# Fox-gMLP trunk, one core: attention's first loads placed inside the last chunk, key weights split earlier, sums and forget rows one tile later

## The chip, the cores and the metric

The kernel runs on one core of one Trainium2 chip. The metric is the device time of one execution in microseconds (us). Before the change the median of three timed runs was 2390.56 us (2388.26 to 2390.97).

A core has five engines that run their own instruction queues: TensorE (PE, matmuls), VectorE (DVE), ScalarE (ACT), GpSimd (POOL) and SyncE (SP). SP computes nothing here; it issues transfers. An engine takes its instructions strictly in the order of its own queue, and waits on semaphores for others.

## The reference

One pre-norm layer for 2048 tokens of width 1024, in float32, and a last RMS norm. What matters here is its first half:

```python
xn = rms_norm(x, mix_norm_g)
h = xn @ w_in                       # 1024 x 2568
q, k, v, f_logit, z = split(h)      # 512, 512, 512, 8, 1024 wide; 8 heads of 64
log_f = log_sigmoid(f_logit + b_f)
c = cumsum(log_f)                   # per head, along the tokens
logit[t, s] = q_t . k_s / 8 + c[t] - c[s],   s <= t
attn = softmax(logit) @ v
sgu  = spatial_gating(gelu(z))      # 128-token chunks
x = x + concat(rms_norm(attn), rms_norm(sgu)) @ w_out
x = x + (silu(gate) * up) @ w_down  # a SwiGLU layer behind it, width 2816
```

## The kernel before

**Precision.** A float32 operand is held as two parts, a rounded one (`h`) and the remainder (`l`). A product is three matmuls: h by h, h by l, l by h. The rounded part of a weight comes from an ACT cast (`wh`, L128), the remainder from a DVE subtraction (`wl`, L131).

**Stage 1** makes q, k, v and the forget gates, for four chunks of 512 tokens. In a chunk, 16 matmuls make the forget logits (L539), then come four query tiles, four key tiles (24 matmuls each, L566, a pair of heads in each) and four value tiles (L460). Chunk 0 has its value tiles first, ahead of the forget logits. ACT, DVE and SP evacuate each tile: scaled, split, and stored to DRAM as `QH`, `QL`, `KH`, `KL`, `VD`. Three generators are advanced once or twice per tile, and what they issue goes between the matmuls:

- `steps` of the next chunk: its x is loaded, split, squared and summed; then `sums` (L285: four matmuls with one column each, that read the summed squares `rb`; DVE and POOL make 1/sqrt of them) and `row` (four transposes, L295).
- `forget_rows`: the chunk's forget logits go through DRAM (`FD`, L549, to the tile `F`), then ACT and DVE make log-sigmoid in the tile `v` (L323 to L331), a transpose (L335), a cumulative sum by matmul (L341), a carry (L345), and a store to `AUG`.
- `max_stream`: row maxima of the logits, ahead of attention. For a head, a chunk of queries and a chunk of keys, four matmuls (L363: tile `D` with keys and AUG rows, tile `A` with queries) and DVE maxima (L365). `D` has four buffers, and its loads run three jobs ahead. The maxima are stored by SP as `md`.

**Stage 2** is attention, mixed with the z projection (L921). A unit is one head and one chunk of queries; a step is one block of 128 keys against it: scores (L729, L730), exp on ACT (L732), p by v (L762 to L767). Its tiles: `load_keys` fills C (KH, KL), D (KH and ten AUG rows) and V; `prep` fills A and B (queries; A also takes the maxima `md`). The remaining `max_stream` runs on in stage 2. The big projections and the SwiGLU layer (L1654) follow.

**What sets the order.** A list scheduler orders every engine's queue when the program is built; `behind(x)` forbids it to place an instruction ahead of x. All loads of stage 2, all loads of `max_stream`, and the stores QL, KL and md are issued by SP, in one queue; POOL loads weights. Before, the first two units' keys and queries were one block behind `k_low[1]`, the store of the last chunk's second key tile:

```python
with behind(k_low[1]):
    for n, u in enumerate(units[:AHEAD]):
        keys_until(0)
        prep(*u, ab)
prep(*units[AHEAD], ab)
xz_in = [ldr(xz0[a], XS[0][:, a, :, 0:P]) for a in range(2)]
```

`xz_in` are the two loads `wsth`, `wstl` for the z projection. `jk` is the buffer for the constant rows `c_row`, which reach DRAM as `CR` and the constant rows of `AUG`; `cm` and `dmask` are constant matrices.

Of the kernel before, what the change touches and what calls it, by code (L numbers as in the profile page):

```python
# [16 lines left out]
P = 128  # L17
# [8 lines left out]
CH = 512  # L26
# [45 lines left out]
FT = 9  # L72
ND = 4
FE = 4
NCH = S // CH
NB = S // P
EPS = 1e-6
# [3 lines left out]
def f(ap):  # L81
    return ap.bitcast(F32)
# [3 lines left out]
def trunk(ctx: ExitStack, tc: tile.TileContext, x, x_t, mix_g, w_in, b_f, ln_g, ln_b, w_st, b_st, on_g, w_out,  # L86
# [55 lines left out]
    tri = cm[:, 0, :]  # L142
    dmask = T(csm, [P, CH], F32, "dmask")

    def load_mats():
        ld(cm, c_mat[:, 128:768].rearrange("p (n q) -> p n q", n=5))
        ld(dmask, c_mat[:, 768:1280])

    ones_c = T(cst, [P, 1], F32, "ones_c")
    onc = T(cst, [P, KT], F32, "onc")  # L150
# [80 lines left out]
    nc.scalar.activation(T(p1, [P, 4], F32, "r1a"), mhalf, AF.Copy, scale=ones_c)  # L231
    CR = T(dram, [34, CH], F32R, "CR")

    def load_const():
        cr = T(p1, [34, CH], F32, "jk", bufs=1)
        ld(cr, c_row)
        crr = T(p1, [34, CH], F32R, "D", bufs=ND)
        nc.vector.tensor_copy(crr, cr)
        ldr(CR, crr)
        a8, a2 = T(p1, [P, 8, P], F32R, "xl", bufs=4), T(p1, [P, 2, P], F32R, "D", bufs=ND)  # L240
        nc.gpsimd.memset(f(a8), 0.0)
        nc.gpsimd.memset(f(a2), -1.0)
        ldr(AUG[:, 0:8, :], a8)
        ldr(AUG[:, 8:10, :], a2)

    class Chunk:
# [51 lines left out]
        def steps(self):  # L298
            self.get(0)
            self.get(1)  # L300
            yield
            for i in range(4):
                self.halves(i)
                self.square(i)
                if i < 2:
                    self.get(i + 2)
                yield
            self.sums()
            yield
            self.row()  # L310
            yield
# [4 lines left out]
    def forget_rows(j):  # L316
# [12 lines left out]
        nc.vector.tensor_tensor(er, er, ru, ALU.mult)  # L329
        nc.vector.tensor_tensor(ln, ln, er, ALU.subtract)  # L330
        nc.vector.scalar_tensor_tensor(lf, F, 0.0, ln, ALU.min, ALU.subtract)  # L331
        for _ in range(2 if j < 2 else 1):
            yield
        pl = T(ps1, [P, 4, P], F32, "tp")
        nc.tensor.transpose(pl[:, 0, :], lf, ident)  # L335
# [112 lines left out]
        return nc.scalar if c else nc.sync  # L448

    last_v = []  # L450
    k_low = deque(maxlen=4)

    def v_open():
        return T(ps1m, [P, CH], F32, "mm", bufs=4)
# [7 lines left out]
    def v_close(pm, xc, tt):  # L462

        v = T(p1, [P, H, P + 1], F32R, "v") if xc.c else T(p1, [P, H, P + 1], F32R, "xh", bufs=4)
        r = r1[:, xc.c * 4 + tt : xc.c * 4 + tt + 1]
        pmv = pm.rearrange("p (h d) -> p h d", h=H)
        (nc.vector if xc.c == NCH - 1 else nc.gpsimd).memset(f(v[:, :, DH : DH + 1]), 1.0)
        a = nc.scalar.activation(v[:, :, 0:DH], pmv, AF.Copy, scale=r)
        nc.vector.scalar_tensor_tensor(v[:, :, P : P + 1], pmv[:, :, 0:1], r, f(v[:, :, 0:1]), ALU.mult, ALU.subtract)
        b = nc.vector.scalar_tensor_tensor(v[:, :, DH + 1 : P], pmv[:, :, 1:DH], r, f(v[:, :, 1:DH]), ALU.mult, ALU.subtract)  # L470
        s = queue(xc.c if xc.c < NCH - 1 or tt < 2 else 0).dma_start(f(VD[xc.c][tt * P : (tt + 1) * P]), f(v))
        if xc.c == NCH - 1 and tt == 1:

            nc.scalar.activation(T(p1, [P, 4], F32, "r1a"), f(v[:, 0, 0:4]), AF.Exp)
        return a, b, s
# [52 lines left out]
            nxt.row()  # L528
    for tt in range(4):
        closed = v_close(pms[tt], nxt, tt)  # L530
    for c in range(NCH):
        xc = nxt
        xh, xl = xc.hi, xc.lo
# [13 lines left out]
        nc.vector.tensor_tensor(fT, fT, xc.rb[0:8], ALU.mult)  # L547
        nc.scalar.activation(fT, fT, AF.Identity, bias=bfc)
        nc.scalar.dma_start(FD[c], fT)  # L549
        gates_ = forget_rows(c)  # L550
        next(gates_)
        n_early = -(-(4 * c * HE[c - 1] + 2) // EB[c]) if c else 0
# [4 lines left out]
        for which, w in ((0, wq), (1, wk)):  # L557
            for pr in range(4):
# [13 lines left out]
                if which == 0:  # L572
                    a = nc.scalar.mul(qh, qs, 0.125)
                    b = nc.vector.scalar_tensor_tensor(ql, qs, 0.125, f(qh), ALU.mult, ALU.subtract)
                    queue(c).dma_start(f(QH[pr][c]), f(qh))
                    s = ldr(QL[pr][c], ql)
                else:
                    a = hi_of(nc.scalar, qh, qs)
                    b = lo_of(nc.vector, ql, qs, qh)
                    queue(c).dma_start(f(KH[pr][c]), f(qh))  # L580
                    s = ldr(KL[pr][c], ql)
                    k_low.append(s)
                if c == which == pr == 0:
                    with behind(a, b, closed[2]):
                        load_mats()
                        load_const()
                        halves_k(0)
                        get_k(2)
                        halves_k(1)
                        get_k(3)  # L590
                if which == (c == 0):
                    xc.keep(pr, b)
                if c == which == 0:
                    with behind(a, b, closed[2]):
                        if pr == 1:
                            halves_k(2)
                        if pr == 2:
                            halves_k(3)
                if c == NCH - 1 and which and pr:
                    with behind(a, b):  # L600
                        halves_z(pr - 1)
# [611 lines left out]
            load_keys(*u, i)  # L1213

    with tc.high_priority():
        with behind(k_low[1]):
            for n, u in enumerate(units[:AHEAD]):
                keys_until(0)
                prep(*u, ab)
        prep(*units[AHEAD], ab)  # L1220
        xz_in = [ldr(xz0[a], XS[0][:, a, :, 0:P]) for a in range(2)]
    zc = z_consts()
    next(zc)
    zg = gates()
# [6 lines left out]
    for n in range(len(steps) + DEPTH):  # L1231
        if n < len(steps):
            h, j, kb = steps[n]
            keys_until(n)
            if n and kb == 0 and units.index((h, j)) + AHEAD < len(units):
                prep(*units[units.index((h, j)) + AHEAD], ab)
            max_due(steps[min(n + 3, len(steps) - 1)][0:2])
# [478 lines left out]
```

## Time and profile before

| | us |
|---|---|
| median of three timed runs | 2390.56 |
| the profiled execution | 2384.64 |
| its span, first to last instruction | 2382.8 |
| PE busy | 2338.7 (98%) |
| DVE busy | 1671.5 (70%) |
| ACT busy | 1055.9 (44%) |
| POOL busy | 627.4 (26%) |
| mean granted TensorE clock | 0.995 of full speed |

Busy is the time in which an engine had an instruction running. The timeline view has one row for an instruction or a group: start, duration, engine, line, operation, output and inputs, and in brackets how long the engine had been idle before, and which instruction ended that wait. The view by windows gives for each stretch the busy time and the number of instructions of PE, its weight loads, DVE, ACT and POOL, then the granted clock, the mean busy share of the 16 DMA engines and GB/s. The view of waits sums an engine's idle times by what ended them: total, number, longest.

### The profile page before, as it was taken

Reading aid. Unit: us, or ns where it says so; the run is one execution under the profiler, and the core shown is the slowest. Engines: PE = TensorE matmul, PEld = TensorE weight load, DVE = VectorE, ACT = ScalarE, POOL = GpSimd, SP = SyncE. Lnnn points to the kernel's source line nnn. Section 1 sums busy time; section 2 is a strip of 40 time slices with the busy share of each in tenths; the row PEclk is TensorE's granted clock in tenths of the full one; section 3 lists DMA queues with packets and bytes.
Section 4 is the critical chain, followed back from the end, with each engine's and each line's share of the span. In section 5 each row is a group of like instructions: output and inputs, shape, how many; then the busy total and the mean of one; then the engine's idle time right before and its main releaser. Section 6 shows DMA issues by size and latency. Waiting matters only on the chain. (4 is left out here: it accounts for less than half of the span.)

```text
span 2382.8 us, 31420 instructions
## 1 busy us (share of the span) xinstructions
PE 2338.7 (98%) x10582; PEld 1893.8 (79%) x10582; DVE 1671.5 (70%) x2736; ACT 1055.9 (44%) x1770; POOL 627.4 (26%) x705
## 2 busy tenths in 40 slices
PE   9999999999999999999999999999999999999997
PEld 7777777777777767888888888788888878888886
DVE  6658658888888666567655656965555696696888
ACT  5322137777778766344323233432323242332433
POOL 1100002122111222221322323232322335364531
PEclk9999999999999999999999999999999999999999
DMA  7845567566587876666233232433232245455453
GB/s 256 286 154 202 196 210 196 165 164 178 154 222 234 225 224 172 211 223 201 71 89 89 80 95 75 153 85 89 72 89 81 81 140 187 167 185 202 152 188 148
DMA packets 358152, 380.60 MB, mean 160 GB/s; under 512 B 22292, under 2 KB 275924, under 8 KB 355432
## 3 DMA queue, kind: packets, MB, share of 16 engines
q1 hardware_dynamic: 342008, 335.36, 46.4%
q0 software_dynamic: 7616, 27.33, 3.3%
q10 hardware_dynamic: 8368, 15.91, 1.8%
q8 instruction: 85, 1.39, 0.2%
q14 instruction: 75, 0.61, 0.1%
HBM read 253.35 MB, written 125.18 MB: 159 GB/s over the span
## 5 line engine op out<-in xcount | busy, mean ns | idle before, releaser
L128 ACT CAST wh<-raw 128x512 fp32r<-128x512 f32 (+2 forms) x492 | 302.3, 621 | 752.7 <-PE pp L1654 607.9
L131 DVE TENSOR_TENSOR wl<-raw,wh 128x512 fp32r<-128x512 f32 (+2 forms) x496 | 374.9, 766 | 80.2 <-ACT wh L128 79.8
L1654 PE MATMUL pp<-wl,wh 128*128 128x512 f32 x1056 | 325.5, 389 | 1.4 <-ACT u L1409 1.2
L1654 PE MATMUL pp<-wh,wh 128*128 128x512 f32 x1056 | 325.3, 389 | 0.0
L1343 POOL TENSOR_TENSOR raw<-raw 128x512 f32<-128x512 f32 (+1 forms) x124 | 165.5, 1336 | 514.9 <-DMA raw<-in_w_gu_dram 334.9
L131 DVE TENSOR_TENSOR Pl<-Pt,Ph 128x512 fp32r<-128x512 f32 (+1 forms) x320 | 194.6, 613 | 79.1 <-ACT Ph L128 76.4
L1654 PEld LDWEIGHTS pp<-wl,wh 128*128 128x128 f32 x1056 | 198.0, 188 | 43.6 <-ACT u L1409 2.1
L1654 PEld LDWEIGHTS pp<-wh,wh 128*128 128x128 f32 x1056 | 198.2, 188 | 41.1
L732 ACT ACTIVATE Pt<-mx_ps 128x512 f32<-128x512 f32 (+1 forms) x320 | 169.3, 534 | 121.6 <-PE mx_ps L730 117.6
L1654 PE MATMUL pp<-wl,wl 128*128 128x512 f32 x528 | 205.7, 390 | 1.0 <-DVE wl L131 0.9
L1654 PE MATMUL pp<-wh,wl 128*128 128x512 f32 x528 | 205.4, 389 | 0.0
L921 PE MATMUL z<-wh,xz 128*128 128x512 f32 x496 | 188.9, 397 | 0.0
L1343 DVE TENSOR_TENSOR raw<-raw,raw 128x512 f32<-128x512 f32 (+1 forms) x112 | 133.8, 1197 | 77.4 <-POOL raw L1343 73.9
L128 ACT CAST Ph<-Pt 128x512 fp32r<-128x512 f32 (+1 forms) x320 | 175.8, 557 | 19.6 <-PE tp L764 3.8
L365 DVE TENSOR_REDUCE mx<-mx_ps 128x1 f32<-128x512 f32 x192 | 130.2, 682 | 23.9 <-PE mx_ps L363 20.4
L742 POOL TENSOR_SCALAR_AFFINE_SELECT Ph<-Ph 128x128 fp32r<-128x128 f32 x128 | 53.0, 414 | 323.0 <-DVE Pl L131 218.6
L363 PE MATMUL mx_ps<-D,A 66*128 66x512 f32 (+2 forms) x320 | 119.6, 376 | 5.7 <-DMA D<-KH 3.0
L762 PE MATMUL tp<-Ph,V 128*128 128x512 f32 (+1 forms) x320 | 118.6, 371 | 4.5 <-POOL Ph L742 3.6
L729 PE MATMUL mx_ps<-A,D 74*128 74x512 f32 (+1 forms) x320 | 118.9, 372 | 2.2 <-ACT Pt L732 2.2
L767 PE MATMUL tp<-Pl,V 128*128 128x512 f32 (+1 forms) x320 | 118.5, 370 | 1.2 <-POOL Pl L742 0.7
L1654 PEld LDWEIGHTS pp<-wl,wl 128*128 128x128 f32 x528 | 99.1, 188 | 22.6 <-DVE wl L131 2.1
L730 PE MATMUL mx_ps<-B,C 128*128 128x512 f32 (+1 forms) x320 | 116.9, 366 | 0.0
(340 smaller groups left out, 5300.9 us busy)
## 6 DMA issues: line engine op xcount, KB each, us to landing
raw<-in_w_gu_dram SPq DMA_DIRECT2D x88, 512.0 KB
xz<-XS SPq DMA_DIRECT2D x31, 1024.0 KB
HD<-hT SPq DMA_DIRECT2D x44, 512.0 KB
D<-KH SPq DMA_DIRECT2D x112, 128.0 KB
XA<-xa SPq DMA_DIRECT2D x27, 512.0 KB
raw<-HD SPq DMA_DIRECT2D x24, 512.0 KB
XA<-xb SPq DMA_DIRECT2D x21, 512.0 KB
xa<-XA SPq DMA_DIRECT2D x20, 512.0 KB
```

The lines of the kernel that those rows point to most:

```text
L128: return nc.scalar.copy(o, i) if eng is nc.scalar else eng.tensor_copy(o, i)
L131: return eng.tensor_tensor(o, i, f(h), ALU.subtract)
L363: last_mx.append(nc.tensor.matmul(pm[:, 0:n], lhs, Dt[0 : lhs.shape[0], 0:n], start=True, stop=True))
L365: nc.vector.tensor_reduce(mx[:, a, s : s + 1], pm, AX.X, ALU.max)
L729: nc.tensor.matmul(st[:, off:], Dt[:, b * P : (b + 1) * P], A[:, off:], start=True, stop=False)
L730: nc.tensor.matmul(st[:, off:], C[:, b * P : (b + 1) * P], B[:, off:], start=False, stop=True)
L732: nc.scalar.activation(Pt[:, off:], st[:, off:], AF.Exp)
L762: nc.tensor.matmul(pv[:, off:], V[:, 0:P], Ph[:, off:], start=kb == 0, stop=False)
L767: nc.tensor.matmul(pv[:, off:], V[:, 0:P], Pl[:, off:], start=False, stop=kb == 4 * j + 3)
L921: nc.tensor.matmul(pz, xz[a][:, k, :], w[b][:, k, :], start=n == 0, stop=n == 3 * KT - 1)
L1343: (nc.vector if e == "v" else nc.gpsimd).tensor_tensor(o, a, b, op)
L1654: nc.tensor.matmul(pm, a[:, k, :], b[:, k, :], start=on is None and k == 0 and e == 0, stop=k == it.kh - 1 and e == 2, skip_group_check=n ...
```

## The change

- **Early loads.** Every store of a query's or key's low part, and the last two value stores of the last chunk, are kept in `stores`; in the last chunk's numbering 0 to 3 are the query tiles, 4 to 7 the key tiles, 8 and 9 the third and fourth value tile. `EARLY` names a store for each load: the first unit's keys and queries stand behind the second query tile's store, the second unit's behind the fourth, the third unit's queries behind the second key tile's, `xz_in` behind the fourth key tile's. All other key loads of the first 32 steps stand behind the third value tile's store.
- **Key weights.** The splits of the first two pieces of the key weights, and the loads of the last two, go from behind chunk 0's first query tile to behind its second value tile.
- **Constants.** `cm` and `c_row` are loaded ahead of chunk 0's query tiles, `dmask` at its fourth query tile; the cast and the stores of `c_row` stay behind the first query tile.
- **One tile later.** Chunk 1's `sums` take one more step, and so does the transpose in chunk 0's forget rows.

```diff
+EARLY = [1, 3, 5, 7, 8]
...
-    def load_const():
-        cr = T(p1, [34, CH], F32, "jk", bufs=1)
-        ld(cr, c_row)
+    def store_const(cr):
         crr = T(p1, [34, CH], F32R, "D", bufs=ND)
         nc.vector.tensor_copy(crr, cr)
...
                 if i < 2:
                     self.get(i + 2)
                 yield
+            if self.c == 1:
+                yield
             self.sums()
...
-        for _ in range(2 if j < 2 else 1):
+        for _ in range((3, 2, 1, 1)[j]):
             yield
         pl = T(ps1, [P, 4, P], F32, "tp")
         nc.tensor.transpose(pl[:, 0, :], lf, ident)
...
-    k_low = deque(maxlen=4)
+    stores = deque(maxlen=10)
...
         s = queue(xc.c if xc.c < NCH - 1 or tt < 2 else 0).dma_start(f(VD[xc.c][tt * P : (tt + 1) * P]), f(v))
+        if xc.c == NCH - 1 and tt >= 2:
+            stores.append(s)
...
         closed = v_close(pms[tt], nxt, tt)
+        if tt == 1:
+            with behind(*closed[:2]):
+                halves_k(0)
+                get_k(2)
+                halves_k(1)
+                get_k(3)
...
         nc.scalar.dma_start(FD[c], fT)
+        if c == 0:
+            cr = T(p1, [34, CH], F32, "jk", bufs=1)
+            ld(cm, c_mat[:, 128:768].rearrange("p (n q) -> p n q", n=5))
+            ld(cr, c_row)
...
-                    s = ldr(QL[pr][c], ql)
+                    stores.append(ldr(QL[pr][c], ql))
...
-                    s = ldr(KL[pr][c], ql)
-                    k_low.append(s)
+                    stores.append(ldr(KL[pr][c], ql))
                 if c == which == pr == 0:
                     with behind(a, b, closed[2]):
-                        load_mats()
-                        load_const()
-                        halves_k(0)
-                        get_k(2)
-                        halves_k(1)
-                        get_k(3)
+                        store_const(cr)
...
                         if pr == 2:
                             halves_k(3)
+                        if pr == 3:
+                            ld(dmask, c_mat[:, 768:1280])
...
-        with behind(k_low[1]):
-            for n, u in enumerate(units[:AHEAD]):
-                keys_until(0)
+        for u, at in zip(units[:AHEAD], EARLY):
+            with behind(stores[at]):
+                load_keys(*u, loads.pop(0)[3])
                 prep(*u, ab)
-        prep(*units[AHEAD], ab)
-        xz_in = [ldr(xz0[a], XS[0][:, a, :, 0:P]) for a in range(2)]
+        with behind(stores[EARLY[2]]):
+            prep(*units[AHEAD], ab)
+        with behind(stores[EARLY[3]]):
+            xz_in = [ldr(xz0[a], XS[0][:, a, :, 0:P]) for a in range(2)]
...
-            keys_until(n)
+            with behind(*[stores[EARLY[4]]] if n < 32 else ()):
+                keys_until(n)
```

The instructions of every engine are the same set in both programs; only their order differs, on PE up to the beginning of stage 2. Three places of the two orders follow (before, then now).

**PE, chunk 0.** `mm_689` is the fourth query tile, `mm_732` (now `mm_728`) the first key tile; `tp_721` (now `tp_762`) is the transpose of the forget rows. Before:

```order
L566 MATMUL mm_689<-xl_258,wh_338 128x512
L566 MATMUL mm_689<-xh_254,wl_339 128x512
L335 MATMUL tp_721<-ident_63,v_628 128x128
L566 MATMUL mm_732<-xh_251,wh_370 128x512
L566 MATMUL mm_732<-xl_255,wh_370 128x512
```

Now:

```order
L576 MATMUL mm_728<-xl_258,wh_370 128x512
L576 MATMUL mm_728<-xh_254,wl_371 128x512
L333 MATMUL tp_762<-ident_63,v_627 128x128
L576 MATMUL mm_773<-xh_251,wh_370 128x512
L576 MATMUL mm_773<-xl_255,wh_370 128x512
```

The transpose went from ahead of the first key tile to behind it, 24 matmuls later. The four one-column matmuls of `sums` went from eight matmuls into the third key tile (`mm_827`) to its end (`mm_810`), 16 matmuls later; before:

```order
L566 MATMUL mm_827<-xh_252,wh_370 128x512
L566 MATMUL mm_827<-xl_256,wh_370 128x512
L285 MATMUL tp_819<-ones_c_67,rb_536 128x1 x4
L566 MATMUL mm_827<-xh_252,wl_371 128x512
L566 MATMUL mm_827<-xh_252,wh_370 128x512
```

Now:

```order
L576 MATMUL mm_810<-xl_258,wh_370 128x512
L576 MATMUL mm_810<-xh_254,wl_371 128x512
L343 MATMUL tp_844<-fT_764,cm_65 128x1
L281 MATMUL tp_853<-ones_c_67,rb_547 128x1 x4
L576 MATMUL mm_861<-xh_251,wh_370 128x512
```

**SP, the last chunk's key tiles.** `D_3062` is a tile of `max_stream`; the rows A and B with the numbers 3437 and 3444 are the second and third unit's queries. Before, the end of the block of stage 2's loads, and what is behind it:

```order
L125 DMA A_3437<-md_1_488_1846 2x512
L125 DMA A_3444<-QH_2_13_76 64x512
L125 DMA A_3444<-CR_248 8x512
L125 DMA B_3447<-QL_2_29_92 64x512
L125 DMA B_3447<-QH_2_13_76 64x512
L125 DMA A_3444<-md_2_714_2772 2x512
L125 DMA md_2_787_3054<-mr_3052 8x128
L125 DMA D_3062<-KH_1_52_115 64x512
L125 DMA D_3062<-AUG_146 2x4x128
L125 DMA KL_3_70_133<-ql_3078 128x512
```

Now:

```order
L126 DMA B_3447<-QH_2_13_76 64x512
L126 DMA A_3444<-md_2_714_2772 2x512
L126 DMA A_3022<-QH_2_21_84 64x512
L126 DMA A_3022<-CR_248 2x512
L126 DMA D_3025<-KH_0_51_114 64x512
L126 DMA D_3025<-AUG_146 2x4x128
L126 DMA md_2_787_3054<-mr_3052 8x128
L126 DMA D_3062<-KH_1_52_115 64x512
L126 DMA D_3062<-AUG_146 2x4x128
L126 DMA KL_3_70_133<-ql_3078 128x512
```

Before, 25 loads of stage 2 stood between `D_3025` and `D_3062`; now none does, and the five of the third unit stand ahead of `D_3025`. The others went up in two groups of nine, ahead of the tiles `D_2780` and `D_2893`.

**SP, early in stage 2.** `D_3958` is a tile of `max_stream`; C, D and V with 865, 870 and 857 are keys and values of the fourth chunk. Before:

```order
L125 DMA xz_3934<-XS_7_70 128x16x128
L125 DMA md_3_1022_3910<-mr_3908 8x128
L125 DMA D_3958<-KH_2_45_108 64x512
L125 DMA D_3958<-AUG_146 2x4x128
L125 DMA A_3988<-QH_1_12_75 64x512
L125 DMA A_3524<-md_3_1022_3910 2x512
```

Now:

```order
L126 DMA xz_3934<-XS_7_70 128x16x128
L126 DMA md_3_1022_3910<-mr_3908 8x128
L126 DMA C_865_3412<-KH_3_46_109 64x512
L126 DMA C_865_3412<-KL_3_62_125 64x512
L126 DMA D_870_3417<-KH_3_46_109 64x512
L126 DMA A_3524<-md_3_1022_3910 2x512
L126 DMA D_870_3417<-AUG_146 10x4x128
L126 DMA V_857_3402<-VD_78_141 128x4x129
L126 DMA D_3958<-KH_2_45_108 64x512
L126 DMA D_3958<-AUG_146 2x4x128
```

Six more transfers now stand ahead of `D_3958`, and one of them reads the maxima that the row above them writes. On PE its first matmul stands 12 rows later than before.

More of the change, by code (lines that the diff above doesn't have):

```diff
@@ L143, in trunk @@
     dmask = T(csm, [P, CH], F32, "dmask")
-    def load_mats():
-        ld(cm, c_mat[:, 128:768].rearrange("p (n q) -> p n q", n=5))
-        ld(dmask, c_mat[:, 768:1280])
     ones_c = T(cst, [P, 1], F32, "ones_c")
```

## The prediction

> **What bounds the kernel now.** I read the page's busy times first, then the view of PE's waits, then the windows around the longest of them, then the timeline at each.
>
> ```profile
> PE 2338.7 (98%) x10582; PEld 1893.8 (79%) x10582; DVE 1671.5 (70%) x2736; ACT 1055.9 (44%) x1770; POOL 627.4 (26%) x705
> ```
>
> PE is busy for all but 44 of 2382.8 us, and the change takes no matmul away. It can only win idle time of PE, or time in which PE's clock was halved. The waits say what there is:
>
> ```profile
> PE pp L1654 <- DVE wl L131: 4.0, 4, 2.3
> PE mx_ps L363 <- DMA D<-KH: 3.0, 1, 3.0
> PE tp L335 <- DVE v L331: 2.3, 1, 2.3
> PE mx_ps L363 <- DVE mx L365: 1.6, 2, 1.3
> PE tp L285 <- DVE rb L280: 1.4, 1, 1.4
> PE mx_ps L363 <- DMA B<-QH: 1.1, 1, 1.1
> ```
>
> The first row lies in the SwiGLU layer, behind everything that moves. The other five are single stalls in stage 1 and at the start of stage 2, in the neighbourhood of the edits. The windows show that they cost more than the waits say:
>
> ```profile
> 50.00:60.00 10.00, 7.70 (x35) 6.07 (x34) 7.79 (x15) 7.22 (x10) 0.92 (x2) 1.00 0.61 187
> 70.00:80.00 10.00, 8.57 (x35) 6.78 (x35) 3.98 (x11) 1.68 (x2) 2.18 (x3) 0.83 0.99 372
> 300.00:310.00 10.00, 10.00 (x47) 8.12 (x45) 8.66 (x20) 1.57 (x2) 1.47 (x2) 1.00 0.97 255
> 310.00:320.00 10.00, 7.11 (x32) 5.42 (x30) 7.38 (x14) 3.19 (x4) 0.92 (x2) 0.99 0.89 269
> 320.00:330.00 10.00, 8.58 (x27) 6.56 (x28) 4.00 (x12) 0.00 (x0) 0.50 (x1) 0.67 0.61 199
> ```
>
> An undisturbed stretch of 10 us holds 47 matmuls. The one from 320 holds 27, with the granted clock at 0.67; behind the stall at 73 us it is 0.83. The stall of 2.30 at 56 left it at 1.00. So a stall is paid twice where the clock drops behind it, and not every stall does that.
>
> **The change part by part: the head.**
>
> ```profile
> 54.67 0.39 PE L566 MATMUL mm<-xl,wh 128*128 128x512 f32 x1
> 54.90 0.39 PE L566 MATMUL mm<-xh,wl 128*128 128x512 f32 x1
> 58.27 0.33 PE L335 MATMUL tp<-ident,v 128*128 128x128 f32 x1 [2.30 <-DVE v L331]
> ...
> 73.42 1.34 PE L285 MATMUL tp<-ones_c,rb 128*128 128x1 f32 x8 [1.43 <-DVE rb L280]
> 74.62 0.77 PE L566 MATMUL mm<-xh,wl 128*128 128x512 f32 x1
> 75.19 0.63 PE L566 MATMUL mm<-xh,wh 128*128 128x512 f32 x1
> ...
> 77.62 0.39 PE L566 MATMUL mm<-xh,wh 128*128 128x512 f32 x1
> ```
>
> A full matmul starts every 0.23 us (54.67, 54.90). *Forget rows.* The transpose wanted to start at 58.27 - 2.30 = 55.97. It now stands 24 matmuls later: 55.97 + 24 x 0.23 = 61.5. Its input was ready at 58.2. One thing makes that input later, the store to FD, which now stands behind the first query tile's split on ACT:
>
> ```profile
> 37.80 0.52 ACTq L549 DMA_DIRECT2D FD<-fT  x1
> 40.41 0.63 ACT L573 ACTIVATE qh<-ql 128x512 fp32r<-128x512 f32 x1 [2.64 <-DVE ql L571]
> 51.70 1.05 ACT L128 CAST wh<-raw 128x1024 fp32r<-128x1024 f32 x1 [4.40 <-DMA raw<-in_w_in_dram]
> ...
> 43.54 0.73 POOL L198 DMA_DIRECT2D raw<-in_w_in_dram  x1 [1.80 <-DVE wl L131]
> ```
>
> It goes from 37.80 to about 41.0, 3.2 us later. If the whole chain moved with it, it would end at 61.4, still in time. It will not: ACT's forget work was queued behind the cast at 51.70, which waited 4.40 us for a piece of the key weights, and that piece's load (43.54) waits for the split of an earlier piece, which now runs some 6 us sooner. I expect the chain to end near 54. Gain 2.30.
>
> *Key weights.* Two casts and two subtractions (1.05 us each on ACT, about 1.2 on DVE) go ahead of the third value tile's evacuation.
>
> ```profile
> 32.84 0.59 ACT L296 COPY rb<-tp 128x512 f32<-128x512 f32 x1 [3.43 <-PE tp L295]
> 43.16 1.22 DVE L131 TENSOR_TENSOR wl<-raw,wh 128x1024 fp32r<-128x1024 f32 x1
> ```
>
> ACT had been idle for 3.43 us there, so they start at once, and the last two value tiles are evacuated 2 to 3 us later. Those PSUM banks are wanted by the third and fourth query tile, at about 45: hidden. Without that cover it would cost those 2 to 3 us.
>
> *Sums.* They wanted to start at 73.42 - 1.43 = 71.99, that is 69.69 without the stall before, and stand 16 matmuls later: 69.69 + 3.7 = 73.4. Their input came at 73.4, so even with no help to DVE the wait is gone. The half clock behind it: from 74.62 to 77.62 seven matmuls start in 3.00 us where 1.60 is normal, so 1.40 more. Gain 1.43 + 1.40.
>
> ```profile
> 75.55 1.10 POOL L288 TENSOR_TENSOR r<-r1a,mhalf 128x4 f32<-128x4 f32 x1
> ```
>
> Late next could be chunk 1's row. POOL's power ended at 76.65 with sums that began at 73.42, as they do now; what reads the sums on DVE now stands behind the third key tile's evacuation there, so it may be 0.5 later. The transposes stand 24 matmuls behind the sums, at 78.9: a margin of 1.7, the narrowest in the head. If it breaks, the cost is what is missing, below 1 us.
>
> **The last chunk.**
>
> ```profile
> 298.85 0.52 SPq L125 DMA_DIRECT2D C<-KH  x1
> ...
> 315.45 0.44 SPq L125 DMA_DIRECT2D A<-md  x1
> ...
> 316.36 0.45 SPq L125 DMA_DIRECT2D D<-KH  x1
> 316.86 0.43 SPq L125 DMA_DIRECT2D D<-AUG  x1
> ...
> 320.08 1.19 PE L363 MATMUL mx_ps<-D,A 66*128 66x512 f32 x2 [2.97 <-DMA D<-KH]
> 323.04 0.80 PE L363 MATMUL mx_ps<-D,A 66*128 66x512 f32 x1 [1.34 <-DVE mx L365]
> ```
>
> SP spent 298.85 to 315.9 on the block of 25 loads, and the maxima's tile `D_3062` was issued only at 316.36. It was wanted at 320.08 - 2.97 = 317.1 and landed 3.2 us after its second issue. With no block between, it is issued 11 us earlier, near 305, behind the third unit's five loads (2.7 us at the spacing of the block). Gain 2.97; the 1.34 behind it came of two jobs' maxima crowded together, and goes too. The half clock: 320 to 330 lacks 47 - 27 = 20 matmuls, 4.26 us at 0.213 each; less 1.34 and the 0.08 of the stall beyond 320, 2.84.
>
> The rows show the clock drop behind waits of 2.97 and of 1.43 (with one-column matmuls behind it), and I count both terms. [...]
>
> Recoverable in all: 2.30 + 1.43 + 1.40 + 2.97 + 1.34 + 2.84 = 12.3.
>
> **What becomes late instead.** The loads of the first two units are now 9 issues ahead of other tiles of the maxima. The tightest is `D_2893`:
>
> ```profile
> 282.98 0.44 SPq L125 DMA_DIRECT2D D<-AUG  x1
> 284.68 0.34 SPq L125 DMA_DIRECT2D QL<-ql  x1
> 296.66 0.40 PE L363 MATMUL mx_ps<-D,A 66*128 66x512 f32 x1
> ...
> 304.70 0.45 SPq L125 DMA_DIRECT2D A<-QH  x1
> 306.84 0.27 SPq L125 DMA_DIRECT2D A<-CR  x1
> ```
>
> It was issued at 282.98 for a matmul at 296.66. Behind the store at 284.68 and nine loads it goes out near 290, or 292 to 293 if SP pauses behind a V load as it did for 2.1 us between 304.70 and 306.84; landing 3.2 us later, at 293 to 296.5. Between 0 and 1 us of stall; I take 0.3.
>
> In stage 2, `D_3958` is now behind C, D and V of the fourth chunk:
>
> ```profile
> 368.51 0.47 PE L363 MATMUL mx_ps<-D,A 66*128 66x512 f32 x1 [1.08 <-DMA B<-QH]
> ...
> 380.62 0.89 SPq L125 DMA_DIRECT2D D<-KH  x1
> 381.56 0.43 SPq L125 DMA_DIRECT2D D<-AUG  x1
> 382.10 0.45 SPq L125 DMA_DIRECT2D A<-QH  x1
> 384.91 0.23 SPq L125 DMA_DIRECT2D A<-md  x1
> ...
> 386.53 0.40 PE L363 MATMUL mx_ps<-D,A 66*128 66x512 f32 x1
> ```
>
> `A<-md` reads the maxima stored just before and went out only at 384.91, some 2.3 us after the issue ahead of it. It now stands ahead of `D_3958`, with two loads between; so that tile goes out at about 386.2 and 386.7, and lands at 386.7 + 3.2 = 389.9. Its matmul, 12 rows later, wants it at 386.53 + 12 x 0.23 = 389.3. Stall 0.6; from 0, if it lands in 2.6, to 2.3 and half a clock window (1.4, as at 74) behind it. I take 1.0.
>
> The wait of 1.08 before 368.51 hangs on loads that keep their neighbours; a few rows of shift decide, 0 to 1.1, and I take 0.5 as gained. The other keys that now stand behind the value tiles are read 15 us or more after their issue, so they are hidden.
>
> **The sum.** 12.3 + 0.5 - 0.3 - 1.0 = 11.5. The profiled execution took 2384.64, 1.84 more than its span, so it should become 2373.1 and the span 2371.3. The timed median was 5.9 above that execution; taken off the median, 2390.56 - 11.5 = **2379** us.
>
> **The rivals.**
>
> *The stall moves.* Both tight tiles come late and the clock drops behind them: `D_2893` 1.0 and `D_3958` 2.3, each with 1.4 to 2.8 of half clock, and no gain at 368. Gain 12.3 - 1.0 - 2.3 - 4.2 = 4.8, so 2385.8. For it: both margins are below 1 us. Against: neither wait would be as long as the 2.97, and the 2.30 at 56 left the clock alone.
>
> *The clock is not the stalls'.* If something else halves it at 74 and 320, the waits alone are won: 2.30 + 1.43 + 2.97 + 1.34 - 0.8 = 7.2, so 2383.4. For it: the stall of 2.30 that left the clock alone, while one of 1.43 did not. Against: the clock is 0.99 or better in every other stretch quoted, and both drops follow a stall at once. [...]
>
> *The change does little.* If the early loads must wait for buffers, SP blocks where they stand and the block of 25 is only shifted, so the last chunk gains nothing; the head's 5.1 less 1.3 of new stalls leaves 3.8: 2386.8. For it: these tiles reuse memory of stage 1. Against: what held the memory before is x and its copies of earlier chunks, long stored.
>
> *Slower.* SP issues in order, and the two groups of nine stand ahead of maxima in a stretch where nothing stalled before.
>
> ```profile
> 272.72 0.45 SPq L125 DMA_DIRECT2D D<-KH  x1
> 287.42 0.40 PE L363 MATMUL mx_ps<-D,A 66*128 66x512 f32 x1
> ...
> 307.81 0.59 SPq L125 DMA_DIRECT2D B<-QH  x1
> 310.08 0.24 SPq L125 DMA_DIRECT2D A<-md  x1
> ```
>
> `D_2780` went out at 272.72 for a matmul at 287.42. Behind nine issues (4.8 us) and a short pause it goes out near 279, so the first group can be held 5 us more before PE feels it; the second has nothing to spare. A hold of 8 us in each, by a V load or a buffer that is still read, makes `D_2780` 3 late and `D_2893` 8, with 2.8 of half clock behind each: 16.6 lost against 12.3, so 2395. It decides from about 6 us. For it: the transfer engines are 97% busy in the quoted window from 300, where the old block ran. Against: the longest pause inside that block was 1.7 (307.81 + 0.59 to 310.08), and the same loads now go out in three smaller groups.
>
> **How the numbers follow.** The forecast (a gain of 8 to 15) has 0.62; the moved stall 0.13; the clock's rival 0.07; little 0.10; slower 0.08. What a measurement of this kernel can tell from no change is 0.2%, 4.8 us. The forecast, the clock's rival and most of the moved stall lie beyond it: faster 0.79. Little, and the rest: same 0.13. Slower 0.08. The low end is a gain of 17: all 12.3, the 1.1, no new stall, and up to 2.8 where a later stall no longer meets the clock. The high end is the case that does little, with 1.2, some half of the 2.7 us by which the timed runs differ among themselves: 2373.5 to 2388.
>
> **What will show it.** Right: in PE's waits no row for L335, L285 or `D<-KH` above 0.5; the granted clock at 1.00 in the windows from 70 and from 320, with 46 or 47 matmuls in the latter; SP's issue of the tile wanted at 317 near 305. Then the whole of stage 2 stands 11 to 12 us earlier with its later waits unchanged. A row for L363 behind a D tile near 287 or 297 (minus 5), or 389 (minus 12), would show the moved stall, and a granted clock under 1 there what it costs. Wrong: a span above 2378 with those waits gone would mean that the time came back later, where the order is unchanged and I see no reason for it.

## The result, and the profile after

| | before | after |
|---|---|---|
| timed beside each other, six runs each, median (us) | 2389.17 (2382.33 to 2390.97) | 2373.65 (2371.03 to 2381.17) |
| ratio of the two, with its 95% interval | | 0.9942 (0.9926 to 0.9959) |
| profiled execution | 2384.64 | 2381.17 |
| its span | 2382.8 | 2379.4 |
| mean granted clock | 0.995 | 0.996 |

The change makes the kernel 0.6% faster. Two things stand out: the profiled execution gained only 3.5 us, a quarter of what the timed runs show, and one wait in it is new. Two more sets of five runs of the same changed kernel, each beside other runs of the kernel before, gave 0.9951 (0.9939 to 0.9963) and 0.9960 (0.9948 to 0.9972). The three together say some 12 us (9.5 to 14).

The view of PE's waits of the changed kernel (total, number, longest):

```profile
PE mx_ps L361 <- issue: 2.0, 1, 2.0
...
PE mx_ps L361 <- DMA B<-QL: 0.2, 1, 0.2
```

The waits for a D tile (3.0), at the forget rows' transpose (2.3) and at the sums (1.4) are gone, and the one at 368 has shrunk from 1.1 to 0.2. A wait of 2.0 at the row maxima (L361, which was L363) has come. The windows say where; behind them stands the same window of 30 us of the kernel before:

```profile
50.00:60.00 10.00, 10.00 (x46) 8.28 (x45) 9.38 (x18) 8.24 (x13) 1.44 (x2) 1.00 0.87 258
70.00:80.00 10.00, 10.00 (x53) 8.40 (x52) 4.26 (x12) 1.24 (x2) 3.26 (x5) 1.00 0.97 359
80.00:90.00 10.00, 7.98 (x33) 5.11 (x32) 2.83 (x6) 2.50 (x4) 1.12 (x2) 0.92 0.65 243
320.00:330.00 10.00, 10.00 (x47) 8.16 (x46) 3.94 (x15) 4.08 (x7) 0.00 (x0) 1.00 0.50 161
...
300.00:330.00 30.00, 30.00 (x135) 24.12 (x135) 21.28 (x53) 8.86 (x13) 2.15 (x3) 1.00 0.68 209
```

```profile
300.00:330.00 30.00, 25.69 (x104) 20.10 (x102) 20.04 (x45) 4.76 (x6) 2.89 (x4) 0.89 0.82 241
```

From 300 to 330 us PE now makes 135 matmuls where it made 104, all at full clock: 31 x 0.213 = 6.6 us. (Rows of 10 us can't be added up for this, since a matmul that crosses a border is counted in both.) From 50 to 80 nothing waits. But the window from 80 holds 33 matmuls for 47. PE's timeline there, and SP's:

```profile
61.34 0.27 PE L333 MATMUL tp<-ident,v 128*128 128x128 f32 x1
72.78 1.03 PE L281 MATMUL tp<-ones_c,rb 128*128 128x1 f32 x8
86.95 0.30 PE L361 MATMUL mx_ps<-D,A 66*128 66x128 f32 x1 [2.02 <-issue]
88.58 0.63 PE L576 MATMUL mm<-xh,wh 128*128 128x512 f32 x1
89.01 0.63 PE L576 MATMUL mm<-xl,wh 128*128 128x512 f32 x1
...
71.51 1.06 SPq L590 DMA_DIRECT2D KH<-qh  x1
72.66 0.38 SPq L126 DMA_DIRECT2D KL<-ql  x1
77.08 1.82 SPq L126 DMA_DIRECT2D D<-KH  x2
79.00 1.54 SPq L590 DMA_DIRECT2D KH<-qh  x1
80.64 0.52 SPq L126 DMA_DIRECT2D KL<-ql  x1
81.25 0.40 SPq L126 DMA_DIRECT2D AUG<-qh  x1
85.49 0.56 SPq L126 DMA_DIRECT2D D<-AUG  x2
```

The transpose and the sums run unhindered, at 61.3 and 72.8. Chunk 1's first row maximum waits 2.02. The view names no releaser ("issue"), but it reads a D tile whose AUG rows were fetched only at 85.49, and in a variant below the view puts the same wait down to `D<-AUG`. The store of those rows went out at 81.25, and SP then stood still for 3.8 us until it had landed. It stands behind the third key tile's stores, and these behind two D loads that went out only at 77.08: by the view of SP's waits they waited 4.0 us for the landing of the keys stored at 71.51. In the kernel before, the same store stood behind the second key tile's:

```profile
74.50 0.41 SPq L125 DMA_DIRECT2D KL<-ql  x1
75.77 0.32 SPq L125 DMA_DIRECT2D AUG<-qh  x1
79.64 1.09 SPq L125 DMA_DIRECT2D D<-KH  x2
```

Behind the wait, matmuls start every 0.43 us (88.58 to 89.01), at half clock (granted 0.50 from 88.41 to 91.83).

### The profile page after: what moved, and what is told of

The parts are those of the page before. It is cut to its first block, busy times and chain, and to the rows that moved or that the text cites. A ratio compares the mean times of both kernels' runs of the same rounds, so it can differ in the third digit from the quotient of the medians.

```text
span 2379.4 us, 31425 instructions
## 1 busy us (share of the span) xinstructions
PE 2340.1 (98%) x10582; PEld 1894.4 (80%) x10582; DVE 1669.8 (70%) x2736; ACT 1055.7 (44%) x1770; POOL 623.3 (26%) x705
## 3 DMA queue, kind: packets, MB, share of 16 engines
q8 instruction: 85, 1.39, 0.3%
## 5 line engine op out<-in xcount | busy, mean ns | idle before, releaser
L363 DVE TENSOR_REDUCE mx<-mx_ps 128x1 f32<-128x512 f32 x192 | 129.9, 682 | 20.5 <-PE mx_ps L361 20.0
L361 PE MATMUL mx_ps<-D,A 66*128 66x512 f32 (+2 forms) x320 | 118.6, 373 | 2.6 <-issue 2.0
```

The costliest lines, as they stand in the source:

```text
L361: last_mx.append(nc.tensor.matmul(pm[:, 0:n], lhs, Dt[0 : lhs.shape[0], 0:n], start=True, stop=True))
L363: nc.vector.tensor_reduce(mx[:, a, s : s + 1], pm, AX.X, ALU.max)
```

## The experiments

My theory after this: the three old stalls and the wait at 368 are gone for the reasons given, and one step of the change, the forget rows one tile later, made a new stall, by a store in SP's queue. The 6 us that the profiled execution lost between 700 and 1050 us, where the order is unchanged, I took for this one execution's. To compare stage 1 of the variants I use the start of attention's first score matmul (L729 before; its number shifts with the edits) in each profile; the waits ahead of it are all that differs.

### The changed kernel again, twice

> The changed kernel once more, nothing edited. Theory (the stalls belong to the order of the program): the first maximum of chunk 1 waits about 2.0 us again near 87 us, with half a window of the clock behind it, no wait at the forget rows' transpose, at the sums, or for a D tile between 280 and 330; up to 700 us the run is again 9 to 10 us ahead of the kernel before. Rival (the stall at 87 us, and the 6 us that the first profile lost between 700 and 1050 us, are the chance of one execution): the wait at 87 us is under 0.5, or is there, but the stretch 700 to 1050 is again lost, then it is the change's. Timed: 2371 to 2376.

2375.22 us (2371.62 to 2378.36), 0.9951 (0.9939 to 0.9963); span of the profile 2369.9. The wait was shorter than expected and had no half clock behind it.

> The changed kernel, nothing edited, on the same chip as the run before, for the comparison. Theory: the wait of 1.2 to 2.4 us at chunk 1's first maximum is there again; the half clock behind it only if the window of the clock's grid around it was less than about 0.4 active. Timed 2371 to 2377. Rival: the wait is absent, so that it is the chance of an execution.

2373.99 us (2372.58 to 2377.32), 0.9960 (0.9948 to 0.9972); span 2370.9. In the timelines, the first run's row and the second's:

```profile
85.47 0.30 PE L361 MATMUL mx_ps<-D,A 66*128 66x128 f32 x1 [1.21 <-issue]
```

```profile
86.68 0.30 PE L361 MATMUL mx_ps<-D,A 66*128 66x128 f32 x1 [1.88 <-issue]
```

The stall belongs to the order: 2.02, 1.21, 1.88. The half clock does not: it fell behind it in the first profile alone (granted clock from 50 to 100 us 0.97 there, 1.00 in the two others). And the windows from 700 to 1100 of the three profiles, in which the order is the same, hold 1843, 1863 and 1872 matmuls:

```profile
700.00:1100.00 400.00, 389.50 (x1843) 308.12 (x1842) 261.65 (x445) 242.87 (x438) 91.00 (x176) 0.99 0.68 205
```

```profile
700.00:1100.00 400.00, 391.51 (x1863) 311.20 (x1862) 267.41 (x449) 244.66 (x440) 91.46 (x173) 1.00 0.69 210
```

```profile
700.00:1100.00 400.00, 391.92 (x1872) 311.40 (x1871) 267.50 (x449) 244.70 (x440) 92.95 (x177) 1.00 0.70 211
```

So roughly 4 to 6 us (20 to 29 matmuls at 0.213; the windows are fixed in time and don't hold quite the same instructions) were lost there in the first execution and not in the others. The two later spans are 12 to 13 us below that of before, as the timed runs are.

### The kernel before again

> The kernel before once more, nothing edited, for a second profile. Theory (stalls belong to the order, but whether the clock drops behind one depends on where it falls in the 3.4 us grid of the granted clock): the waits at the transpose, the sums and near 317 are there again within 0.7 us each, and the half-clock windows need not be the same ones; the clock drops behind a window of that grid in which PE was active less than about 0.4 and behind no other. Rival: other stalls than before, or drops behind windows that are more than half active.

2385.35 us (2382.79 to 2389.52), 1.0001 (0.9992 to 1.001). Its waits at the transpose and for a D tile are there again; the one at the sums is not. The rows of PE's waits, and of the timeline at the transpose:

```profile
PE mx_ps L363 <- DMA D<-AUG: 3.2, 1, 3.2
PE tp L335 <- DVE v L331: 2.2, 1, 2.2
...
57.92 0.33 PE L335 MATMUL tp<-ident,v 128*128 128x128 f32 x1 [2.22 <-DVE v L331]
```

The clock was halved from 59.3 to 62.7 here (granted 0.50), behind a stall of 2.22 that in the first profile (2.30) left it alone. The sums then came late enough not to wait. So I had one number wrong in my expectation (the sums' wait within 0.7), and for a reason that shows how these stalls hang together: time lost at one gives slack to the next.

### The early loads alone

```diff
 # before.py, with the early loads of the change and nothing else of it
+        for u, at in zip(units[:AHEAD], EARLY):
+            with behind(stores[at]):
+                load_keys(*u, loads.pop(0)[3])
                 prep(*u, ab)
...
```

> The kernel before with the early loads alone (the four stores they hang on, and the keys behind the third value tile); key weights, constants, sums and forget rows as before. Theory: waits of 2.3 at the transpose and 1.4 at the sums with the half clock at 74 us stay, no D tile waits between 280 and 330, and stage 2 starts 7 us earlier: 7 to 8 us under the kernel before. Rival (the loads only move the stall to the maxima they now precede): waits of 1 us or more near 287 or 297, and less than 3 us gained.

2377.10 us (2375.91 to 2385.85), 0.9968 (0.9956 to 0.9981): 7.6 us gained. The two head stalls stay, and no wait stands between 280 and 330:

```profile
57.65 0.33 PE L336 MATMUL tp<-ident,v 128*128 128x128 f32 x1 [2.02 <-DVE v L332]
73.08 1.05 PE L286 MATMUL tp<-ones_c,rb 128*128 128x1 f32 x8 [1.71 <-DVE rb L281]
```

The first score matmul starts at 323.46, against 330.70 and 329.26 in the two profiles of before. The theory holds; the loads did not move the stall.

### The head alone

```diff
 # after.py, with the loads of stage 2 as before, the later keys too
-        for u, at in zip(units[:AHEAD], EARLY):
-            with behind(stores[at]):
-                load_keys(*u, loads.pop(0)[3])
+        with behind(stores[5]):
+            for n, u in enumerate(units[:AHEAD]):
+                keys_until(0)
                 prep(*u, ab)
...
```

> The changed kernel with the early loads undone: one block of stage 2's loads behind the last chunk's second key tile, other keys as before; key weights, constants, sums and forget rows as changed. Theory: the first 100 us are those of the changed kernel (some 2 us gained), and the wait of about 3 us for a D tile near 317 with the half clock behind it stays; so 2 to 3 us under the kernel before. Rival (the early loads matter little, the head shifts the rest): within 3 us of the changed kernel.

2384.16 us (2381.72 to 2388.41), 0.9994 (0.9985 to 1.0002): 1.4 us, not told from none. The stall before the second job's maxima is there, in PE's timeline:

```profile
316.98 1.19 PE L361 MATMUL mx_ps<-D,A 66*128 66x512 f32 x2 [3.72 <-DMA D<-AUG]
319.42 0.79 PE L361 MATMUL mx_ps<-D,A 66*128 66x512 f32 x1 [0.82 <-DVE mx L363]
```

The first score matmul starts at 327.11. The two parts alone add to 9 us, the whole to 12; the difference is within their intervals.

### One group again

```diff
-EARLY = [1, 3, 5, 7, 8]
+EARLY = [5, 5, 5, 5, 8]
```

> The changed kernel with the first two units' keys and queries, the third's queries and the z weights all behind the second key tile's store again, the other keys behind the third value tile as changed: the loads ahead of D_3062 are one block of 23, against 25 before. Theory (the one block on SP's queue made the stall): a wait of 2 us or more for a D tile between 305 and 320 us and 3.4 or 6.8 us of half clock behind it; 5 to 8 us above the changed kernel. Rival (moving the other keys behind the value tiles is what freed the queue): no wait above 0.5 there, within 2 us of the changed kernel.

2382.85 us (2378.93 to 2385.18), 0.9988 (0.9979 to 0.9998): 7.6 to 9.2 us above the changed kernel's three medians, a little more than the 5 to 8 expected. PE's waits, and the window of 30 us:

```profile
PE mx_ps L361 <- DMA D<-KH: 3.0, 1, 3.0
...
300.00:330.00 30.00, 24.84 (x99) 19.56 (x98) 18.91 (x44) 5.02 (x7) 2.16 (x3) 0.89 0.76 224
```

With the other keys behind the value tiles as in the change, but the first units' loads in one block, the stall is back with its half clock, and the first score matmul starts at 329.78. The trace has 25 loads in this block (296.86 to 313.82), as many as before, and not 23: the two groups of nine leave out two loads of ten AUG rows, which in the changed kernel go out at 294.35 and 294.69, behind the last AUG store. So what wins the last chunk is that the block was taken apart and most of it moved ahead, and not the later loading of the rest. Whether the smaller groups or their earlier places did it isn't told apart: no run moved the whole block ahead in one piece.

### The key weights back

```diff
 # after.py
-        if tt == 1:
-            with behind(*closed[:2]):
-                halves_k(0)
-                get_k(2)
-                halves_k(1)
-                get_k(3)
...
                         store_const(cr)
+                        halves_k(0)
+                        get_k(2)
+                        halves_k(1)
+                        get_k(3)
```

> The changed kernel with the key weights' splits and loads back behind the first query tile; sums and forget rows stay one tile later, early loads stay. Theory of the prediction (the 24 and 16 matmuls of delay alone take the two waits away: inputs at 58.2 and 73.4 in the kernel before, new slots at 61.4 and 73.4): no wait above 0.3 at the transpose, at most 0.5 at the sums; the stall near 85 us stays between 1 and 2; within 1.5 us of the changed kernel. Rival (the delays need the earlier weights, which free ACT and DVE): waits of 1 us or more at the transpose or the sums, the half clock behind them, and 3 us or more above the changed kernel.

2377.16 us (2376.47 to 2379.12), 0.9971 (0.9960 to 0.9981): 2 to 3.5 us above the changed kernel's three medians. The ratio's interval overlaps two of the changed kernel's three and just misses the third, so this is likely and not settled. In PE's timeline:

```profile
68.06 0.49 PE L339 MATMUL tp<-cm,fT 128*128 128x128 f32 x2 [1.22 <-DVE fT L336]
88.82 0.40 PE L361 MATMUL mx_ps<-D,A 66*128 66x128 f32 x1 [2.39 <-DMA D<-AUG]
```

The waits at the transpose and the sums are gone, as the prediction had it without help from the weights. But the next step of the forget rows, the cumulative sum (L339), now waits 1.22 for VectorE's copy, and the first maximum 2.39, with half a clock window behind it (88.9 to 92.3; granted clock 0.97 from 50 to 100, and full speed in the matmul rows up to 82). The first score matmul starts at 323.74, later than in all three profiles of the changed kernel (319.17 to 321.70). The theory was right on the two waits it spoke of and wrong on the cost: it stopped one step too early in the chain.

### Both delays back

```diff
 # after.py
-            if self.c == 1:
-                yield
...
-        for _ in range((3, 2, 1, 1)[j]):
+        for _ in range(2 if j < 2 else 1):
```

> The changed kernel with both one-tile delays undone: sums and forget rows at their old places, key weights split early, early loads as changed. Theory: the forget chain is ready at 54.1 for a slot at 55.9, so no wait there; the sums' input comes at about 70.3 for a slot at 69.7, a wait of 0.5 to 1.0 with the one-column matmuls; no stall at chunk 1's first maximum, none at its row: 0 to 2 us from the changed kernel, on either side. Rival (the delays are what won the head): waits of 2.0 and 1.4 come back with the half clock, and 4 us or more are lost in the first 100.

2372.97 us (2372.24 to 2375.54), 0.9955 (0.9943 to 0.9968): the changed kernel's time. No wait at the transpose or at the maxima; the one at the sums is

```profile
70.61 1.05 PE L281 MATMUL tp<-ones_c,rb 128*128 128x1 f32 x8 [1.22 <-DVE rb L276]
```

It is a little longer than the 0.5 to 1.0 expected, and the clock was halved behind it, from 71.70 to 75.12 (granted 0.97 from 50 to 100; matmuls start every 0.42 to 0.43 us from 71.94 to 74.92, and every 0.23 from 75.25). The first score matmul starts at 320.90, among the changed kernel's three. So with the key weights split early, the two one-tile delays together win nothing that can be measured: the one takes the wait at the sums away, the other brings the wait at the first maximum.

### The forget rows back, and a head without waits

```diff
 # after.py
-        for _ in range((3, 2, 1, 1)[j]):
+        for _ in range(2 if j < 2 else 1):
```

> The changed kernel with one edit undone: chunk 0's forget rows are transposed at their old place, ahead of the first key tile. In the changed kernel their input was ready at 54.1, and the old slot is at 55.9. Theory (the new stall at 87 us comes from the AUG store, which came one tile later and stood behind the third key tile's stores in SP's queue): no wait at the transpose, none at chunk 1's first maximum, granted clock 1.00 from 80 to 95 us, so about 3 us less than the changed kernel: 2369 to 2372. Rival (the transfer engines are 97% busy from 70 to 80 us, so the rows of AUG land late wherever their store stands): the wait near 87 us stays above 1.5, and the time is that of the changed kernel within 1 us.

2374.55 us (2371.84 to 2376.45), 0.9947 (0.9935 to 0.9959). The stall at the first maximum is gone, so it came of the store's place; the rival, that full transfer engines make the rows late anyhow, falls. The first score matmul starts at 318.61, 0.6 to 3.1 us ahead of the changed kernel's three profiles. But the 2369 to 2372 expected were missed: the median is the changed kernel's. The 3 us had counted a half clock that the changed kernel showed in one profile of three, and a wait has come at chunk 1's row, in PE's timeline:

```profile
79.92 0.65 PE L291 MATMUL tp<-ident,r 128*128 128x128 f32 x4 [0.93 <-POOL r L284]
```

VectorE read the sums only at 77.32, behind the third key tile's low part; that started at 76.71, when ACT's cast was done, after 3.38 of idle time on VectorE. What that cast had waited for was not shown in this variant; I took it for a buffer that an earlier KH store was still reading, as a cast at 84.80 in the changed kernel's first profile had waited 10.61 for `KH<-qh`. The next variant reads them ahead of it:

```diff
 # in addition to the edit above
+                ahead = c == 0 and which and pr == 2
+                if ahead:
+                    with behind(mm):
+                        next(xg, None)
                 qh = T(p1, [P, CH], F32R, "qh")
...
-                between(a, b, mm)
+                if ahead:
+                    with behind(a, b, mm):
+                        next(gates_, None)
+                else:
+                    between(a, b, mm)
```

> The changed kernel with two edits: chunk 0's forget rows at their old place, and chunk 1's sums read on VectorE ahead of the third key tile's low part (the program advances the next chunk's generator before that tile's evacuation, not behind it), so that POOL's power comes in time for the row. Theory: of the three waits that were seen between 50 and 100 us in the variants (forget rows, sums, chunk 1's first maximum or its row) none above 0.3 remains; the first 100 us are 0.9 to 1.2 us shorter than with the forget rows alone put back, and as the clock can no longer drop there, the timed median is 1 to 3 us below the changed kernel's: 2370 to 2373. Rival (the transfer engines' load from 70 to 90 us makes one instruction late whatever the order): another wait of about 1 us appears behind it, and the time is the changed kernel's within 1 us.

2371.86 us (2367.74 to 2375.44), 0.9948 (0.9936 to 0.996); beside it the changed kernel had 0.9960 (0.9948 to 0.9972). One wait is left from 50 to 100, where none above 0.3 was expected:

```profile
61.83 0.49 PE L339 MATMUL tp<-cm,fT 128*128 128x128 f32 x2 [0.68 <-DVE fT L336]
```

The first score matmul starts at 318.31, the earliest of all profiles (the changed kernel's three: 321.70, 319.17, 320.29), but only 0.3 us ahead of the variant with the forget rows alone put back, for 0.9 to 1.2 expected: one wait went, another came. It has the lowest median, 2 us below the changed kernel beside it, but the intervals overlap: it beats the kernel before, and whether it beats the changed one is not settled.

## Why the prediction was right

The time of 2373.65 lies at the low end of the range (2373.5 to 2388), 5 us under the forecast of 2379; the gain that the forecast rested on, 11.5 us, was close: the ratios give 9.5 to 14, the two later profiles 12 to 13. That the time lies inside the range is luck: the low end is called a gain of 17, but the terms named for it add up to 12.3 + 1.1 + 2.8 = 16.2, which is 2374.4, and the measured time is below that.

**The last chunk: right, in place and size.** The sum had 2.97 + 1.34 + 2.84 = 7.15; the window of 30 us shows 6.6, and with the loads alone the first score matmul starts 7.2 earlier and the time is 7.6 lower. The D tile wanted at 317 was to go out near 305. It did (first the tile ahead of it, then the first issue for it):

```profile
302.69 0.45 SPq L126 DMA_DIRECT2D D<-AUG  x1
...
305.71 0.45 SPq L126 DMA_DIRECT2D D<-KH  x1
```

**The half clock: right in the main.** The clock's rival, that the half clock is not the stalls', falls for the last chunk: with the stall near 317 the half clock stayed (one group, head alone, both profiles of before: granted clock 0.89 from 300 to 330), without it it went (all others: 1.00). That a stall of a given length has it or not is another matter, and the last section comes to it.

**The forget rows and the sums: right on the two waits, incomplete behind them.** The chain was to end near 54; its last instruction ended at 53.84 + 0.29:

```profile
53.84 0.29 DVE L329 SCALAR_TENSOR_TENSOR v<-F,v 128x128 f32<-128x128 f32 x1
```

The step that failed is the claim that chunk 1's row, with a margin of 1.7, is "the narrowest in the head". The row did not wait in the changed kernel; a place that the prediction had not looked at did. I followed the sums one step on, to POOL and the transposes, but not the forget rows to their own end: the store to AUG, its place in SP's queue, and the D tile that reads it. That was the one place where the delay of a tile had a price: 1.2 to 2.0 us, and a half-clock window in one profile of three. In matmuls from 50 to 100 us (204 before), the three profiles have 214, 226 and 223: 2.1, 4.7 and 4.0 us, for 5.1 in the sum. The price I put on the key weights' part, nothing but hidden work, missed that they shorten the rest of the forget rows: by the medians of the run without them, 2 to 3.5 us, which is likely and not settled.

**What becomes late instead: mis-sized, on the safe side.** I charged 0.3 for `D_2893` and 1.0 for `D_3958`. Both went out where I had them, and neither made PE wait; in SP's and PE's timelines:

```profile
292.72 0.44 SPq L126 DMA_DIRECT2D D<-AUG  x1
295.02 0.40 PE L361 MATMUL mx_ps<-D,A 66*128 66x512 f32 x1
...
377.10 0.43 SPq L126 DMA_DIRECT2D D<-AUG  x1
380.54 0.40 PE L361 MATMUL mx_ps<-D,A 66*128 66x512 f32 x1
```

At 295 the rows had landed within 2.3 us of their issue, where I took the 3.2 of another place. At 380 PE came 3.4 us after the issue, where I had it come 2.6 after: the landing may well be the 3.2, and the margin is thin. The wait at 368 gave 0.9, for 0.5.

**The sum and the median.** The 12.3 called recoverable, less a new stall of 2.0 with half a clock window (1.7), of 1.2, or of 1.9, is 8.6, 11.1 and 10.4; the first score matmul, at 330.70 in the first profile of before, starts 9.0, 11.5 and 10.4 earlier in the three profiles, and 12.4 earlier in the head without the new stall. So the terms up to there, taken together, hold within half a microsecond. One reading was off without consequence: the row of waits "1.6, 2, 1.3" is two stalls and not a single one; the sum took the 1.34 from the timeline. That the median came out lower than 2379 is not in these terms: I subtracted from a median of three runs, 2390.56. The kernel before had medians of 2389.17 (six runs, those three among them), 2386.60, 2385.85 and 2384.03 beside the four sets of other kernels. The first of these takes 1.4 of the 5 us; why the sets differ, and why the first ratio gives a larger gain than the other two, stays open.

**The sign of being wrong.** A span above 2378 with the waits gone was to mean that time came back later, and the first profile, with 2379.4, shows just that. The two later ones, 2369.9 and 2370.9, show that it was that execution's and not the change's. Two halved clock steps, the last section's 842.8 and 873.5, cost up to 1.7 us each of it (half of 3.41); the rest stays open.

**The rivals.** The slower one and the one that does little fall with the loads alone. The stall did move, though not where I looked: to SP's queue in the head and not to the D tiles of the last chunk.

## What to carry to other kernels

When a step is delayed on purpose, follow what it feeds to the end, through the stores and the queue they stand in, and not only to the instruction that had waited. A block of loads in a queue that also feeds the running stage is better taken apart and put where the stage's own next loads have time to spare; here nine at a time were hidden in such places, 25 in one block were not, in three kernels. And where a profile differs from the timed runs by more than what is being weighed, take a second profile before explaining the difference.

## What the runs showed of the hardware

The granted clock is 1.00 or 0.50 in the first profiles of the kernel before and of the changed one, and from one change of it to the next it is a whole number of steps of 3.413 us. In the kernel before it was halved from 74.02 for one step, from 319.78 for two and from 1958.18 for one, with 71, 478 and 121 steps at full clock behind them; in the changed kernel from 88.41, 842.76, 873.48 and 1955.50, one step each, with 220, 8, 316 and 121 behind them. So in these traces the changes lie on a grid, and two stalls of nearly the same length, 2.30 and 2.22, fell differently in it and did not both have a halved step behind them. The windows below are steps of that grid; first the kernel before, first profile, then its second:

```profile
53.54:56.95 3.41, 2.43 (x11) 1.69 (x9) 3.41 (x8) 3.08 (x5) 0.72 (x1) 1.00 0.38 69
56.95:60.37 3.42, 2.10 (x10) 1.76 (x11) 3.42 (x7) 2.30 (x4) 0.57 (x1) 1.00 0.88 283
316.37:319.78 3.41, 0.73 (x4) 0.27 (x2) 2.10 (x3) 1.62 (x2) 0.00 (x0) 1.00 0.94 303
```

```profile
55.89:59.30 3.41, 1.38 (x7) 1.16 (x8) 3.41 (x8) 2.81 (x4) 0.00 (x0) 1.00 0.86 269
59.30:62.71 3.41, 3.41 (x10) 2.65 (x9) 2.89 (x6) 2.19 (x3) 0.71 (x1) 0.50 0.88 297
```

The stall of 2.30 lay across two steps, which kept 11 and 10 matmuls of the 15 that fit (3.41 / 0.23), and the clock stayed at 1.00, up to 74.02. The stall of 2.22 lay within one, which kept 7, and the next step was at 0.50.

I counted each matmul with 0.23 us for 512 columns in the full-clock steps of the first profiles of before and of the changed kernel, 689 and 688 up to PE's last matmul. The clock fell behind the steps in which PE was active for a share of 0.17, 0.24 and 0.36 (from 316.37, 1954.77 and 70.61 in the kernel before) and of 0.25, 0.37, 0.39 and 0.39 (from 1952.09, 839.35, 85.00 and 870.07 in the changed one), and behind no other. Of the steps that kept it one had 0.385 (from 1522.01 in the changed kernel), which is just below the two of 0.39 (0.389 and 0.393); all others had 0.42 or more. So here a stall need not fill a step (7 matmuls stood in the one from 85.00), and what went with the drop was not the one wait but all the time of a step in which PE did little. The waits of 1.43 and 1.22 at the sums had a halved step behind them (from 74.02 before, from 71.70 with both delays back), and there eight one-column matmuls, 1.34 and 1.05 us long, stood next to the wait. In these two profiles a step that lost less than 0.6 of its length, 2.05 us, kept the clock, and of the eight that lost more seven had a halved step behind them; a halved step may cost up to another 1.7 us, an estimate from half of 3.41.

This is also part of the scatter among executions of one program. Up to 1900 us the first profile of the changed kernel had halved steps at 88.4, 842.8 and 873.5. Of its other two profiles one had a halved step near the last of these (867.1, behind a step from 863.70 with 4 matmuls), and neither had the first two, though the waits ahead of them were there in all three: 2.02, 1.21 and 1.88 at the first maximum, and between 833 and 843 us 1.29, 0.89 and 0.57 in the first profile, 1.39, 0.92 and 0.58 in the second, 1.29, 0.89 and 0.57 in the third.
